# A hybrid attention and retention block on one core: operand halves loaded and split in place, ten gate tiles, a second projection in smaller pieces, and three small moves of order

## Chip, cores and metric

The kernel runs on one core of one Trainium2 chip. The metric is the device time of one execution in microseconds (us). The core has five engines that work side by side, each on its own queue of instructions in a fixed order: TensorE (PE) multiplies matrices, VectorE (DVE) and ScalarE (ACT) work on elements, GpSimd (POOL) takes some small work, and SyncE (SP) issues the transfers (DMA). Engines wait for each other by semaphores. Operands lie in SBUF, PE's results in PSUM, and what does not fit goes to DRAM.

## The reference

One decoder block in float32, 1024 tokens of width 1024:

```python
xn = rmsnorm(x, norm1_g)
qa, ka, va, qr, kr, vr, gr, gate_a, gate_b = split(xn @ w_in)
o_a = dilated window attention (3 groups x 4 heads, mixed)      # S x 512
o_r = head_groupnorm(retention(qr, kr, vr)) * silu(gr)          # S x 2048, 4 heads
y = sigmoid(gate_a) * (o_a @ w_proj_a) + sigmoid(gate_b) * (o_r @ w_proj_b)
x = x + y @ w_out
xn2 = rmsnorm(x, norm2_g)
x = x + square(relu(xn2 @ w_up)) @ w_down
```

The query and key heads are normalised too (`q_norm_g`, `k_norm_g`); that takes a root per head and token.

## The kernel before

**Split operands.** Every float32 operand is split into a high part (`xh`, `wh`, an ACT copy, line 350) and a low part (`xl`, `wl`, the difference, a DVE instruction, line 353). A product takes three matmuls for each pair of 128 rows: high by high, high by low, low by high (line 247, tiles of 128x512).

**Stages.** In order: heads and their norms, attention, retention (four heads of eight chunks, c = 0 to 7), the first projection (`w_proj_a`, tag `pa`), the second (`w_proj_b`, tag `pb`), the output projection, norm, `up`, `down`. The last retention head overlaps with the first projection: PE works on both in turn.

**Products with seven multiplications.** `pb`, `up` and `down` multiply 2x2 blocks with seven products instead of eight (N1 to N7, `product`). The weights of a unit j come as two raw tiles and are split into pieces A, D, B, C; between D and B, DVE makes four sums of raw blocks in place (line 124). On the data side the sums of blocks of the retention's output are made by POOL and DVE, stored in DRAM (`on_d`, line 1021) and read back by halves (512 KB). After N1 ACT copies the result to a second PSUM bank (line 419), after N6 it copies the bank out (line 424), after N7 too (line 427), and PE needs that bank again soon.

**What sets the order.** PE's order is written out by hand. The other engines' instructions are ordered by a scheduler, apart from those that are pinned to the program's order (`keep_in_program_order`). `W` plans the weights: a list of splits, each with a raw load (line 185); `W.lag`, `W.pace` and `W.limit` say how far ahead of use a split is made, and `W.tick`, called after each `pipe.step`, makes the next one. `pipe.at(n, fn)` calls a function n steps later. A tile's load cannot be issued before the last reader of the tile's old content is done; SP's queue waits there, with all that stands behind.

**Buffers around the change.** The attention's output (`oa_d`) and the blocks of the retention's output (`on_d`) are loaded into `oraw` tiles (pool `pr`, three buffers, 512 KB each; lines 905 and 945) and split from there into the operand pairs: `xh_95`/`xl_96`, `xh_97`/`xl_98` (the attention's output), `xh_7928`/`xl_7929` (N5) and `xh_99`/`xl_100` (N7). Until then these pairs hold the normalised input, from which PE makes the last head's values. The gates of the first projection are loaded into `s0` tiles, four in pool `pm2` (line 898, sigmoid in line 909 or 1103, product with PE's result in line 1104, store in line 1105); later ones into pieces of an operand's tile that is not yet needed (`spare`). In the second projection parts for the later half of the units are loaded as quarters (256 KB) into `s` tiles, up to six under way, and split three products later; its results pass through `result`, which adds and multiplies with a gate, and `keep`, which splits them as operands of the output projection.

**Heads' root.** Line 821 takes the square root of the mean squares of four heads at once (`work<-mean`). Root and sigmoid (line 862) are in different tables of ACT, so each change of function loads a table.

Of the kernel before, what the change touches and what calls it, by code (L numbers as in the profile page):

```python
# [17 lines left out]
P = 128  # L18
# [19 lines left out]
class Weights:  # L38
# [38 lines left out]
    def add(self, src, buf=None):  # L77
# [10 lines left out]
        def step():  # L88
            h, l = self.buffer(buf)
            self.split(h[:, :w], l[:, :w], self.raw[r][:, :w])  # L90
            self.units[n] = h, l
            self.used.add(r)
# [4 lines left out]
    def add_units(self, tag, srcs, flip=0):  # L97
# [8 lines left out]
        def piece(key, buf, r, cols, then=None):  # L106
            def step():
# [6 lines left out]
                self.split(h, l, self.raw[r][:, cols], key[0] == "up" and key[1] < 2 and key[2] != "A")  # L114
# [6 lines left out]
        def sums(r):  # L121
            (x22, x21), (x11, x12) = ((self.raw[i][:, 0:512], self.raw[i][:, 512:1024]) for i in (r, r - 1))
            for x, y in ((x22, x21), (x21, x11), (x11, x22), (x12, x11)):
# [106 lines left out]
class Pipe:  # L230
# [25 lines left out]
    def step(self, ps, terms, ends=None, first=True):  # L256
# [14 lines left out]
        self.tick()  # L271
# [25 lines left out]
def hybrid_block(ctx: ExitStack, tc: tile.TileContext, a: dict, out: bass.AP):  # L297
# [51 lines left out]
    def split(dst_h, dst_l, src, pin=False):  # L349
# [3 lines left out]
        nc.vector.tensor_tensor(dst_l, src, dst_h.bitcast(F), op=OP.subtract)  # L353
# [34 lines left out]
    for nb in range(2):  # L388
        for u in range(4):
            W.add(a["w_out"][nb, u], (4, 3, 5, 2)[u] if nb else (0, 1, 5, 2)[u])  # L390
# [9 lines left out]
    def product(tag, j, name, unit, operands, pu, result):  # L400
# [13 lines left out]
        pipe.step(u[bank], terms, None, fresh)  # L414
# [378 lines left out]
    with ExitStack() as ph:  # L793
# [16 lines left out]
        def add(n):  # L810
# [6 lines left out]
            if n == HEADS - 1:  # L817
# [3 lines left out]
                nc.scalar.activation(w, y, AF.Sqrt)  # L821
# [79 lines left out]
    def load_sum(from_, c, name, h):  # L901

        raw = from_.tile([P, 2, 512], F, name="oraw")
        o = 2 * SUMS.index(name)
        nc.sync.dma_start(raw, on_d[2 * c + h, o:o + 2].rearrange("k p t -> p k t"))
        return raw

# [3 lines left out]
    def part_sum(to, raw, h):  # L911

        split(*(x[:, 2 * h:2 * h + 2] for x in to), raw, True)

    ret = ExitStack()
    with ExitStack() as ph:
# [26 lines left out]
        def load_oa(s):  # L943
            raw = pr.tile([P, S], F, name="oraw")
# [3 lines left out]
        for h in range(RH):  # L948
# [4 lines left out]
            for c in range(NT):  # L953
# [119 lines left out]
                if h == RH - 1 and c == NT - 1:  # L1073
                    W.lag, W.pace = 2, 1
                    raws = [(name, g, load_sum(pr, 0, name, g), -3) for name, g in (("N5", 0), ("N5", 1), ("N7", 0))]


    with ExitStack() as ph:
        ES, e1, exts = None, ExitStack(), ExitStack()
        OPB = [{"N5": XS[0, 1], "N7": XS[1, 1]}, {}]  # L1080
        waiting = [("N7", 1)] + [(name, h) for name in ("N1", "N2", "N4", "N6") for h in range(2)]
        spare = []
        sigmoid(gates[0])
        for n, (d, cs) in enumerate(work):
# [6 lines left out]
            for _ in range(2 if len(gates) < n + 8 else 0):  # L1091
                if spare:
                    e, es = work[len(gates)]
                    gates.append(spare.pop(0))
                    nc.sync.dma_start(gates[-1], sg_d[0, e, :, es])
# [3 lines left out]
            if n < len(work) - 1:  # L1099
                s0 = gates[n + 1]  # L1100
                if s0 in places:
                    gates[n + 1] = pm2.tile([P, 512], F, name="s0")
                tc.keep_in_program_order(nc.scalar.activation(gates[n + 1], s0, AF.Sigmoid))
            nc.vector.tensor_tensor(gates[n], gates[n], pp, op=OP.mult)
            nc.sync.dma_start(pa_d[d, :, cs], gates[n])
            if ES is None and not pipe.due:
# [5 lines left out]
                places = [x[:, k].bitcast(F) for x in ES[3] for k in range(4)]  # L1112
                spare = list(places)
# [3 lines left out]
            if raws and raws[0][0] in OPB[0] and raws[0][3] <= n - 2:  # L1117
                name, h, raw, _ = raws.pop(0)
                part_sum(OPB[0][name], raw, h)
            if waiting and waiting[0][0] in OPB[0] and (n % 2 or n > 11) and len(raws) < 3:  # L1120
                name, h = waiting.pop(0)
# [515 lines left out]
```

## Time and profile before

| | |
|---|---|
| three runs | 2178.85, 2179.03, 2179.24 us; median 2179.03 |
| profiled execution | 2176.74 us, its span 2175.0 us |
| PE busy, granted clock | 2151.6 us (99%), full |
| DVE, ACT, POOL busy | 1356.0, 1098.4, 316.0 us |
| data moved by DMA | 358.81 MB, mean 165 GB/s |

By stage, from windows of the profile (us from the span's start):

| stretch | what runs | length | PE busy | DVE | ACT | DMA share |
|---|---|---|---|---|---|---|
| 400 to 430 | heads' norms | 30 | 29.39 | 17.11 | 14.53 | 0.30 |
| 1195 to 1265 | last retention head from chunk 4 on | 70 | 69.50 | 55.75 | 44.48 | 0.52 |
| 1265 to 1305 | first projection | 40 | 38.53 | 24.77 | 20.08 | 0.88 |
| 1305 to 1450 | second projection | 145 | 140.99 | 116.32 | 78.36 | 0.79 |
| 1450 to 1545 | its end, output projection | 95 | 93.92 | 49.12 | 33.17 | 0.45 |
| 1545 to 1580 | start of up | 35 | 32.97 | 30.25 | 22.72 | 0.25 |
| 1580 to 2175 | up and down | 595 | 589.86 | 400.64 | 311.06 | 0.52 |

A row of the timeline reads: start, duration, engine, line, operation, output<-input, shape, count; in brackets the engine's idle time just before it and what ended it. A row of the list of waits reads: engine, tile and line that waited, what ended the wait; then us in total, times, the longest. Successive matmuls overlap, so their durations add up to more than PE's time.

### The profile page before, as it was taken

What the parts mean: (1) busy time and instruction counts of PE and PEld (TensorE: products, weight loads), DVE (VectorE), ACT (ScalarE), POOL (GpSimd) and SP (SyncE); (2) the same over time, 40 slices, a digit from 0 to 9 for tenths busy, and PEclk for the clock granted to TensorE, in tenths of its full rate; (3) what the DMA queues carried; (4) which work ended last, traced back from release to release, by engine and by line L of the source; (5) the groups of instructions that cost most, each with busy time, mean ns of one, the idle gap of its engine ahead of it and who ended that gap; (6) DMA issues with size and microseconds to landing.
All of it is one profiled execution on the core that took longest, in us unless ns stands there. A gap on an engine that the chain in (4) does not pass through costs nothing. (4 is left out here: it accounts for less than half of the span.)

```text
span 2175.0 us, 28668 instructions
## 1 busy us (share of the span) xinstructions
PE 2151.6 (99%) x9928; PEld 1764.2 (81%) x9928; DVE 1356.0 (62%) x2327; ACT 1098.4 (51%) x2097; POOL 316.0 (15%) x340
## 2 busy tenths in 40 slices
PE   9999999999999999999999999999999999999999
PEld 6887777788888888888888877778788888888887
DVE  5723443565556665657776767783865556788884
ACT  5425555444655554545555655552654545755552
POOL 1000000000000000002123120000000000777773
PEclk9999999999999999999999999999999999999999
DMA  6323333333658676664364487774255556745443
GB/s 210 133 82 93 109 104 102 100 130 120 202 170 241 199 222 191 199 200 140 110 193 121 128 288 268 259 239 154 88 150 160 151 146 204 235 152 191 166 140 107
DMA packets 294579, 358.81 MB, mean 165 GB/s; under 512 B 35025, under 2 KB 202385, under 8 KB 294178
## 3 DMA queue, kind: packets, MB, share of 16 engines
q1 hardware_dynamic: 293890, 356.72, 52.4%
q8 instruction: 78, 1.28, 0.2%
q14 instruction: 67, 0.55, 0.1%
q10 hardware_dynamic: 544, 0.26, 0.0%
HBM read 240.33 MB, written 116.59 MB: 164 GB/s over the span
## 5 line engine op out<-in xcount | busy, mean ns | idle before, releaser
L353 DVE TENSOR_TENSOR wl<-raw,wh 128x1024 fp32r<-128x1024 f32 (+1 forms) x308 | 343.0, 1115 | 462.6 <-ACT wh L350 461.5
L350 ACT ACTIVATE wh<-raw 128x1024 fp32r<-128x1024 f32 (+1 forms) x308 | 296.0, 963 | 297.9 <-PE ms L247 106.6
L247 PE MATMUL mm<-xh,wh 128*128 128x512 f32 x960 | 387.7, 404 | 2.3 <-ACT ms L419 2.2
L247 PE MATMUL mm<-xl,wh 128*128 128x512 f32 x960 | 374.2, 390 | 0.9 <-DVE xl L353 0.9
L247 PE MATMUL mm<-xh,wl 128*128 128x512 f32 x960 | 375.0, 391 | 0.0
L247 PE MATMUL ms<-xh,wh 128*128 128x512 f32 x784 | 318.0, 406 | 4.5 <-ACT u L427 2.9
L247 PE MATMUL ms<-xh,wl 128*128 128x512 f32 x784 | 306.2, 391 | 1.4 <-DVE wl L353 1.4
L247 PE MATMUL ms<-xl,wh 128*128 128x512 f32 x784 | 305.6, 390 | 0.0
L247 PEld LDWEIGHTS mm<-xh,wl 128*128 128x128 f32 x960 | 180.2, 188 | 39.6 <-DVE wl L353 0.7
L247 PEld LDWEIGHTS mm<-xh,wh 128*128 128x128 f32 x960 | 180.5, 188 | 37.4 <-ACT ms L419 3.0
L247 PEld LDWEIGHTS mm<-xl,wh 128*128 128x128 f32 x960 | 180.7, 188 | 35.3 <-DVE xl L353 1.3
L247 PE MATMUL mm<-wh,xh 128*128 128x512 f32 x458 | 186.1, 406 | 0.1
L247 PEld LDWEIGHTS ms<-xh,wh 128*128 128x128 f32 x784 | 147.4, 188 | 45.2 <-issue 10.1
L999 POOL TENSOR_TENSOR st<-st,half 128x1 f32<-128x1 f32 x32 | 25.8, 807 | 1075.6 <-DVE st L998 1075.6
L247 PE MATMUL mm<-wh,xl 128*128 128x512 f32 x458 | 179.6, 392 | 0.9 <-DVE xl L353 0.9
L247 PE MATMUL mm<-wl,xh 128*128 128x512 f32 x458 | 178.5, 390 | 0.0
L247 PEld LDWEIGHTS ms<-xh,wl 128*128 128x128 f32 x784 | 147.1, 188 | 33.7 <-DVE wl L353 1.8
L247 PEld LDWEIGHTS ms<-xl,wh 128*128 128x128 f32 x784 | 147.6, 188 | 26.9
L247 PEld LDWEIGHTS mm<-wh,xl 128*128 128x128 f32 x458 | 86.0, 188 | 20.6 <-DVE xl L353 1.4
L247 PEld LDWEIGHTS mm<-wh,xh 128*128 128x128 f32 x458 | 86.2, 188 | 16.1 <-ACT xh L350 0.6
L247 PEld LDWEIGHTS mm<-wl,xh 128*128 128x128 f32 x458 | 86.5, 189 | 15.7
L247 PE MATMUL ms<-wh,xh 128*128 128x512 f32 x232 | 92.3, 398 | 0.0
(309 smaller groups left out, 3827.9 us busy)
## 6 DMA issues: line engine op xcount, KB each, us to landing
raw<-in_w_up SPq DMA_DIRECT2D x32, 512.0 KB, 3.8
h_d<-s SPq DMA_DIRECT2D x64, 256.0 KB, 4.3
raw<-in_w_down SPq DMA_DIRECT2D x32, 512.0 KB, 3.5
raw<-in_w_aqk_q SPq DMA_DIRECT2D x24, 512.0 KB, 3.5
qk_d<-sg SPq DMA_DIRECT2D x48, 256.0 KB, 3.0
qk<-qk_d SPq DMA_DIRECT2D x24, 512.0 KB, 5.8
rb<-rs_d SPq DMA_DIRECT2D x24, 512.0 KB, 7.1
xh<-h_d SPq DMA_DIRECT2D x11, 896.0 KB, 4.6
```

What stands on the lines that cost most here:

```text
L247: self.nc.tensor.matmul(ps, x, y, start=start, stop=stop, skip_group_check=not first)
L350: hi = nc.scalar.activation(dst_h, src, AF.Copy)
L353: nc.vector.tensor_tensor(dst_l, src, dst_h.bitcast(F), op=OP.subtract)
L999: nc.gpsimd.tensor_tensor(st[:, 9:10], st[:, 8:9], half[:, 0:1], op=OP.pow)
```

## The change

1. **Operand parts split in place.** The pool `pr` goes. A half (`load_half`, and `load_oa`) is loaded into the low tile of its own target and split from there: `xh <- xl`, then `xl <- xl - xh`. The splits are pinned and made three steps after the load's step.
2. **Ten gate tiles.** `pm2` has ten buffers; all gates are loaded into them, up to eight ahead, and the sigmoid always writes in place.
3. **Finer second projection.** Its parts come as halves like the others, one a product. For units j > 1 the four sums are made two at a time, and the splits are pinned. The weights' tick comes after the parts of a product have been dealt with, not inside it; the lag is 3. The last results' steps are pinned or held back to the end (`last`).
4. **Heads' root behind a copy.** The root is made one step later, pinned; reciprocals and what follows too.
5. **Up's third weight piece later.** The limit before `up` is one lower and is raised at (0, N2).
6. **Pacing ended sooner.** `W.lag` and `W.pace` are reset in `up` at the last unit but one, N6.

```diff
@@ add_units @@
+                late = key[0] == "pb" and key[1] > 1
-                self.split(h, l, self.raw[r][:, cols], key[0] == "up" and key[1] < 2 and key[2] != "A")
+                self.split(h, l, self.raw[r][:, cols], late or key[0] == "up" and key[1] < 2 and key[2] != "A")
...
+                fine = tag == "pb" and j > 1
-                piece((tag, j, "D"), (self.D, j % 2), r, slice(0, 512), lambda r=r: sums(r))
+                piece((tag, j, "D"), (self.D, j % 2), r, slice(0, 512), None if fine else lambda r=r: sums(r))
+                if fine:
+                    self.steps += [(set(), r, lambda r=r, k=k: sums(r, k)) for k in ((0, 1), (2, 3))]
@@ the heads' norms @@
-                nc.scalar.activation(w, y, AF.Sqrt)
+                pipe.at(1, lambda: tc.keep_in_program_order(nc.scalar.activation(w, y, AF.Sqrt)))
...
-                    pipe.at(2 + c, lambda c=c: invert(slice(P * c, P * c + P)))
-                pipe.at(6, refine)
+                    pipe.at(3 + c, lambda c=c: invert(slice(P * c, P * c + P)))
+                pipe.at(7, refine)
@@ loads of the parts @@
-    def load_sum(from_, c, name, h):
-
-        raw = from_.tile([P, 2, 512], F, name="oraw")
-        o = 2 * SUMS.index(name)
-        nc.sync.dma_start(raw, on_d[2 * c + h, o:o + 2].rearrange("k p t -> p k t"))
-        return raw
...
-    def part_sum(to, raw, h):
-
-        split(*(x[:, 2 * h:2 * h + 2] for x in to), raw, True)
+    def load_half(at, c, name, h):
+
+        xh, xl = (x[:, 2 * h:2 * h + 2] for x in OPB[c][name])
+        o = 2 * SUMS.index(name)
+        nc.sync.dma_start(xl.bitcast(F), on_d[2 * c + h, o:o + 2].rearrange("k p t -> p k t"))
+        begun.append((at, xh, xl))
+
+    def split_halves(upto):
+
+        while begun and begun[0][0] <= upto:
+            _, xh, xl = begun.pop(0)
+            split(xh, xl, xl.bitcast(F), True)
...
-            raw = pr.tile([P, S], F, name="oraw")
+            raw = oaS[s][1].bitcast(F)
...
-                    pr = pool(load, "pr", 3)
-                    pm2 = pool(load, "pm2", 4)
+                    pm2 = pool(load, "pm2", 10)
...
-                    raws = [(name, g, load_sum(pr, 0, name, g), -3) for name, g in (("N5", 0), ("N5", 1), ("N7", 0))]
+                    for name, g in (("N5", 0), ("N5", 1), ("N7", 0)):
+                        load_half(-3, 0, name, g)
@@ first projection, step n @@
-            if len(gates) == n + 3 and n + 3 < len(work):
-                e, es = work[n + 3]
+            while len(gates) < min(n + 8, len(work)):
+                e, es = work[len(gates)]
                 gates.append(loaded(pm2, sg_d[0, e, :, es], "s0"))
...
-                s0 = gates[n + 1]
-                if s0 in places:
-                    gates[n + 1] = pm2.tile([P, 512], F, name="s0")
-                tc.keep_in_program_order(nc.scalar.activation(gates[n + 1], s0, AF.Sigmoid))
+                sigmoid(gates[n + 1])
...
+            split_halves(n - 3)
+            if waiting and waiting[0][0] in OPB[0] and (n % 2 or n > 11):
+                load_half(n, 0, *waiting.pop(0))
@@ second projection @@
+            if n == len(results) - 1 and n in ahead and not done:
+                done.append(n)
+                last.append(lambda: result(j, f, cs, src))
+                return
...
+            elif j > 5 and cs.start and n < len(results) - 1:
+                last.append(lambda: keep(j, f, cs, y))
...
+        W.lag = 3
...
             product("pb", j, name, unit, OPB[j // 4], lambda: parts, result)
-            todo += [(1, after[j, name], k) for k in range(4) if (j, name) in after]
+            pipe.tick()
+            todo += [(1, after[j, name], h) for h in range(2) if (j, name) in after]
...
+            split_halves(base + i - 3)
+            if todo:
+                load_half(base + i, *todo.pop(0))
@@ before and in up @@
-    W.limit = W.first["up"] + 5
+    W.limit = W.first["up"] + 4
...
-            if (j, name) in ((1, "N2"), (0, "N5")):
-                W.limit = W.limit + 1 if j else len(W.steps) - 11 * (NC - 1)
+            if (j, name) in ((0, "N2"), (1, "N2"), (0, "N5")):
+                W.limit = W.limit + 1 if name == "N2" else len(W.steps) - 11 * (NC - 1)
...
+            if (j, name) == (NU - 2, "N6"):
+                W.lag, W.pace = 0, None
```

PE's and POOL's instructions keep their order. In what follows a line number of the changed kernel stands some 5 to 13 above that of the same line before (350 becomes 356, 994 becomes 1007). First ACT in the heads' norms, before and after (`work<-mean` is the root, `u<-ms` the copy after N7, `sg<-` the sigmoids):

```order
L350 ACTIVATE wh_3067<-raw_2789 128x1024
L821 ACT_TABLE_LOAD
L821 ACTIVATE work<-mean 128x512
L427 ACTIVATE u_3048<-ms 128x512
L862 ACT_TABLE_LOAD
L862 ACTIVATE sg<-u_3048 128x512
L862 ACTIVATE sg<-mm 128x512
```

```order
L356 ACTIVATE wh_3067<-raw_2789 128x1024
L435 ACTIVATE u_3047<-ms 128x512
L870 ACTIVATE sg<-u_3047 128x512
L829 ACT_TABLE_LOAD
L829 ACTIVATE work<-mean 128x512
L870 ACT_TABLE_LOAD
L870 ACTIVATE sg<-mm 128x512
```

The copy and one sigmoid now stand ahead of the root and its table load.

Second, ACT at the end of the last retention head, before and after (`on` is the copy of the head's output that is normalised, `Sh` the state's high part, `smh` that of the scores, `onT` the transposed output, `s0` a gate's sigmoid):

```order
L350 ACTIVATE xh_7928<-oraw_11258 128x1024
L994 ACTIVATE on_11200<-ms_11190 128x512
L350 ACTIVATE Sh_11222<-St_10410 128x512
L350 ACTIVATE wh3_11378<-raw2_11176 128x512
L350 ACTIVATE Sh_11222<-St_10410 128x512
L1103 ACTIVATE s0_11036<-s0_11036 128x512
L350 ACTIVATE smh_11239<-sm_11237 128x128
L350 ACTIVATE vh_11250<-mm_11140 128x512
L350 ACTIVATE xh_7928<-oraw_11260 128x1024
L350 ACTIVATE wh5_11425<-raw0_11182 128x512
L1031 ACTIVATE onT_11278<-tr_11273,gng_106 128x128 x4
L1103 ACTIVATE s0_11138<-s0_11138 128x512
```

```order
L356 ACTIVATE xh_7928<-xl_7929 128x1024
L1007 ACTIVATE on_11194<-ms_11184 128x512
L356 ACTIVATE xh_7928<-xl_7929 128x1024
L356 ACTIVATE wh3_11376<-raw2_11170 128x512
L356 ACTIVATE Sh_11216<-St_10407 128x512 x2
L910 ACTIVATE s0_11031<-s0_11031 128x512
L356 ACTIVATE vh_11244<-mm_11134 128x512
L356 ACTIVATE wh5_11420<-raw0_11176 128x512
L910 ACTIVATE s0_11132<-s0_11132 128x512
L356 ACTIVATE xh_99<-xl_100 128x1024
L356 ACTIVATE smh_11233<-sm_11231 128x128
L1044 ACTIVATE onT_11272<-tr_11267,gng_106 128x128 x4
```

The split of N5's second half has moved ahead of the state's parts, and that of N7's first half, which stood behind `onT` and a sigmoid, ahead of `smh`.

Third, SP in the same place, before and after:

```order
L185 DMA raw0_11182<-in_w_pa 128x512
L185 DMA raw1_11337<-in_w_pa 128x512
L1021 DMA on_d_85<-onE_10736 128x4x128
L1021 DMA on_d_85<-onT_11152 128x4x128
L1021 DMA on_d_85<-n6_11158 128x2x128
L905 DMA oraw_11389<-on_d_85 128x2x512
```

```order
L919 DMA xl_7929<-on_d_85 128x2x512
L190 DMA raw0_11176<-in_w_pa 128x512
L919 DMA xl_7929<-on_d_85 128x2x512
L1034 DMA on_d_85<-onE_10733 128x4x128
L1034 DMA on_d_85<-onT_11146 128x4x128
L1034 DMA on_d_85<-n6_11152 128x2x128
L190 DMA raw1_11331<-in_w_pa 128x512
L919 DMA xl_100<-on_d_85 128x2x512 x2
```

Before, the load in this place was that of N7's second half; N5's halves and N7's first had been issued between chunks 4 and 6. Now all four stand here, each behind PE's last reading of its target.

More of the change, by code (lines that the diff above doesn't have):

```diff
@@ L254, in group, with step @@
                 after(i)
-    def step(self, ps, terms, ends=None, first=True):
+    def step(self, ps, terms, ends=None, first=True, tick=True):
         fns = self.due.pop(self.slot, [])
@@ L1087, in hybrid_block @@
                 uh, ul = W[ua]
-            if len(gates) == n + 3 and n + 3 < len(work):
-                e, es = work[n + 3]
+            while len(gates) < min(n + 8, len(work)):
+                e, es = work[len(gates)]
                 gates.append(loaded(pm2, sg_d[0, e, :, es], "s0"))
[L1091 to L1095, printed above, removed]
+                if len(gates) > n + 5:
+                    break
             pp = ms.tile([P, 512], F, name="ms")
@@ L1154, in fetch, with keep @@
             ahead[n] = [loaded(pm3, src[d, :, cs], "s") for src in srcs]
-        def keep(j, f, cs, y):
+        last, done = [], []
+        def keep(j, f, cs, y, pin=False):
             yh, yl = (x[:, f, cs] for x in as_rows(YS[j - 4]))
-            split(yh, yl, y)
+            split(yh, yl, y, pin, pin)
         def result(j, f, cs, src):
@@ L1191, in hybrid_block @@
         fetched = {order[order.index(at) - 3]: u for at, u in free.items()}
-        todo, unit = [(c, name, k) for c, name in ((0, "N3"),) for k in range(4)], {}
-        begun = []
-        def load_part(c, name, k):
-            return loaded(pm3, on_d[2 * c + k // 2, 2 * SUMS.index(name) + k % 2], "s")
+        todo, unit, base = [(0, "N3", h) for h in range(2)], {}, len(work)
+        W.lag = 3
         fetch(0)
@@ L1221, in hybrid_block @@
         W.pump()
+        for fn in last:
+            fn()
         e1.close()
```

54 lines of the change are left out of this document (23 added, 31 removed).

## The prediction

> **What bounds the kernel now.** I read the page's busy time first, then TensorE's (PE's) list of waits, then the timeline round each wait.
>
> ```profile
> span 2175.0 us, 28668 instructions
> PE 2151.6 (99%) x9928; PEld 1764.2 (81%) x9928; DVE 1356.0 (62%) x2327; ACT 1098.4 (51%) x2097; POOL 316.0 (15%) x340
> PE ms L247 <- ACT u L427: 2.9, 4, 1.2
> PE mm L247 <- ACT ms L419: 2.2, 2, 1.4
> PE mm L247 <- DVE xl L353: 1.8, 2, 0.9
> PE ms L247 <- DVE s L1104: 1.5, 2, 1.2
> PE ms L247 <- DVE wl L353: 1.4, 1, 1.4
> ```
>
> PE is busy 99% of the span, and the change leaves its instructions and their order as they are. So only PE's waits can move the time. The five rows add up to 9.8 us; that is nearly all that this change can touch and win. The profiled execution took 2176.74 us, 1.74 more than its span and 2.29 less than the median of the runs, 2179.03. I make the sum on 2176.74 and carry the difference to the median. A shift under 0.2% (4.4 us) I count as no change.
>
> After a wait the next 128x512 matmul takes 0.50 us where its neighbours take 0.39 (rows below), so removing a wait wins its length and 0.1.
>
> **Gains, part by part.** *The heads' root.*
>
> ```profile
> 416.36 1.28 ACT L821 ACT_TABLE_LOAD   x1
> 417.66 0.63 ACT L821 ACTIVATE work<-mean 128x512 f32<-128x512 f32 x1
> 418.19 0.58 ACT L427 ACTIVATE u<-ms 128x512 f32<-128x512 f32 x1
> 418.82 0.50 PE L247 MATMUL ms<-xh,wh 128*128 128x512 f32 x1 [0.61 <-ACT u L427]
> ```
>
> ScalarE (ACT) takes table load and root ahead of the copy at L427 that empties PE's accumulator. Afterwards the copy and one sigmoid stand first. What is late then is the root, and its readers (reciprocals on VectorE, DVE) are moved one step later too. Gain 0.6 + 0.1 = 0.7.
>
> *Ten gate tiles.* In the first projection a gate's sigmoid (L1103) and product (L1104) wait until an earlier store frees their tile:
>
> ```profile
> 1285.68 0.63 ACT L1103 ACTIVATE s<-xh 128x512 f32<-128x512 f32 x1 [2.69 <-DMA pa_d<-s]
> 1286.34 0.69 DVE L1104 TENSOR_TENSOR s<-s,ms 128x512 f32<-128x512 f32 x1 [2.09 <-ACT s L1103]
> 1287.08 0.50 PE L247 MATMUL ms<-xh,wh 128*128 128x512 f32 x1 [1.23 <-DVE s L1104]
> ```
>
> With ten tiles the sigmoids run in place and no store stands in front; the last gates are loaded six steps ahead. Both waits on L1104 go: 1.5 + 2 x 0.1 = 1.7.
>
> *Operand splits, second projection.* Its start and its two waits on L427 look alike: splits stand ahead of the copy that PE needs.
>
> ```profile
> 1306.69 1.06 ACT L350 ACTIVATE xh<-oraw 128x1024 fp32r<-128x1024 f32 x1 [0.25 <-DMA oraw<-on_d]
> 1307.66 1.06 ACT L419 ACTIVATE ms<-mm 128x512 f32<-128x512 f32 x2
> 1308.29 0.50 PE L247 MATMUL mm<-xh,wh 128*128 128x512 f32 x1 [1.35 <-ACT ms L419]
> 1328.05 0.50 PE L247 MATMUL ms<-xh,wh 128*128 128x512 f32 x1 [0.41 <-ACT u L427]
> 1405.86 0.50 PE L247 MATMUL ms<-xh,wh 128*128 128x512 f32 x1 [0.70 <-ACT u L427]
> ```
>
> Afterwards only one split, of a part loaded some 3 us before, stands ahead of L419, with about 1 us to spare: gain 1.4. At 1328 the split moves behind the copy: 0.5. At 1405.86 a split of 128x1024 (1.06) replaces two of half that size, but a weight's split no longer stands ahead of it; I leave 0.2 of the wait and take 0.6.
>
> *Finer second projection.* The low half of a weight waits in DVE's queue:
>
> ```profile
> 1438.79 0.69 DVE L353 TENSOR_TENSOR xl<-s,xh 128x512 fp32r<-128x512 f32 x1
> 1439.40 2.36 DVE L353 TENSOR_TENSOR wl<-raw,wh 128x1024 fp32r<-128x1024 f32 x2
> 1440.67 0.50 PE L247 MATMUL ms<-xh,wl 128*128 128x512 f32 x1 [1.42 <-DVE wl L353]
> 1466.16 0.50 PE L247 MATMUL mm<-wh,xl 128*128 128x512 f32 x1 [0.94 <-DVE xl L353]
> ```
>
> With the sums drawn apart, 11 half-size DVE steps (the first row and the next start 0.61 apart), ACT's split (1.06) and the low half (half of 2.36) follow the product that starts them: 6.7 + 1.1 + 1.2 = 9.0. PE's 38 matmuls up to this weight's use take 38 x 0.23 = 8.7 (one starts 0.23 after the other in the timeline). I leave 0.4 of the wait and take 1.1. At the output projection's start the last weight splits end about 3 us before PE needs the results' low halves: the wait of 0.94 and a small one before it go, 1.2.
>
> Gains: 0.7 + 1.7 + 1.4 + 0.5 + 0.6 + 1.1 + 1.2 = 7.2. If the tight places keep half their waits it is 5.5; with none left, 8.0.
>
> **Edits that I cost at nothing.** *Up's third weight piece.*
>
> ```profile
> 1559.39 1.99 ACT L350 ACTIVATE wh<-raw 128x1024 fp32r<-128x1024 f32 x2
> 1562.92 0.49 PE L247 MATMUL mm<-xh,wh 128*128 128x512 f32 x1 [0.83 <-ACT ms L419]
> 1562.17 2.35 DVE L353 TENSOR_TENSOR wl<-raw,wh 128x1024 fp32r<-128x1024 f32 x2
> 1573.40 0.69 DVE L1267 TENSOR_TENSOR x<-x,x 128x512 f32<-128x512 f32 x1
> 1574.66 1.07 ACT L1360 ACTIVATE q<-mm 128x512 f32<-128x512 f32 x2
> 1575.29 0.49 PE L247 MATMUL mm<-xh,wh 128*128 128x512 f32 x1
> ```
>
> The second of the two splits moves behind the copies at L419, so PE starts 0.9 sooner at 1562. But from 1562.17 to the addition that ends at 1574.09 DVE has no gap, and its work up to there is the same in another order. ACT's squares (L1360) still begin at 1574.66 behind a split of that addition, and PE, ahead by 0.9, waits for them at 1575.29. The gain is given back: 0, with 0.9 as the upper end.
>
> *Pacing ended sooner.* Nothing moves in any queue from there on. The wait that it could have meant stays:
>
> ```profile
> 1861.14 0.50 PE L247 MATMUL ms<-xh,wh 128*128 128x512 f32 x1 [1.15 <-ACT u L427]
> ```
>
> **Losses: the loads into the operands themselves.** Before, halves came into a ring of their own, long before their split. Now a load writes the low operand's tile, and SyncE (SP) may issue it only when PE has finished with that tile. The splits stand in ACT's and DVE's in-order queues at nearly the old places, ahead of the last retention head's own steps.
>
> ```profile
> oraw<-on_d SPq DMA_DIRECT2D x6, 512.0 KB, 4.0
> DMA to landing us min/median/max: 3.7/5.0/6.0
> 1198.72 1.04 ACT L350 ACTIVATE xh<-oraw 128x1024 fp32r<-128x1024 f32 x1
> 1202.78 0.58 ACT L994 ACTIVATE on<-ms 128x512 f32<-128x512 f32 x1
> 1213.08 0.61 ACT L994 ACTIVATE on<-ms 128x512 f32<-128x512 f32 x1
> 1243.07 0.60 ACT L994 ACTIVATE on<-ms 128x512 f32<-128x512 f32 x1
> 1248.14 0.45 SPq L905 DMA_DIRECT2D oraw<-on_d  x1
> 1248.54 0.31 ACT L350 ACTIVATE smh<-sm 128x128 fp32r<-128x128 f32 x1
> 1249.11 0.63 PE L1026 MATMUL tr<-ident,on 128*128 128x128 f32 x4
> 1253.54 0.60 ACT L994 ACTIVATE on<-ms 128x512 f32<-128x512 f32 x1
> ```
>
> I take 4.0 us from issue to landing, the median for this stretch (first row), with 3.7 and 6.0 as ends.
>
> *Chunks 4 and 5.* PE frees the first target near 1198.7, where the split used to start. Load and split end near 1204, so the normalising copy (L994) ends at about 1204.6 instead of 1203.4. About 1.2 us of slack follow before PE transposes it, leaving 0.3. In chunk 5 two splits, a gate's sigmoid and its table load stand ahead of the copy at 1213.08: it slips by some 2.2 against a slack of 0.8, leaving 1.4. Together 1.7; ends 0.5 and 3.6.
>
> *The end of the head.* The first half of N5 is issued after PE's read near 1239.1, lands near 1243, and its split pushes the copy of 1243.07 to 1244.5. DVE, with both halves' low parts (1.23 each) ahead of the normalisation, is ready for the transposes of 1249.11 about 1.3 late; 0.1 of this stood there before. The first half of N7 stands in SP's queue behind three stores and a weight load, is issued near 1248.7 and lands near 1252.7. Its split stands in ACT's queue ahead of `smh` of 1248.54, `onT` and the copy of 1253.54, which then ends near 1256.3 where PE wants it near 1255.2 (already slipped); behind it the gate product and both low halves of the state are late by 0.7, 0.4 and 0.5. In all 1.2 + 1.1 + 0.7 + 0.4 + 0.5 = 3.9, less 0.4 of waits that were there: 3.5; ends 2.2 and 6.4.
>
> Losses 1.7 + 3.5 = 5.2; 2.7 to 10.0.
>
> [...]
>
> **Sum.** 2176.74 - 7.2 + 5.2 = 2174.7 for an execution like the profiled one; plus 2.29, 2177.0 for the median.
>
> **Rivals.**
>
> 1. *The loads land soonest and hurt little* (faster). If they land in 3.7 us and each split keeps its slack, the losses are 2.7, the gains 8.0, and the time is 2179.03 - 5.3 = 2173.7. For it: SP and the DMA engines are not full in this stretch. Against it: one load stands behind three stores, and two waits are DVE's order rather than the landing.
> 2. *The late loads decide* (slower). The place is ACT's queue at the end of the last retention head. If the halves land at 6.0, the longest row, they cost 10.0; with the gains at 5.5 the time is 2179.03 + 4.5 = 2183.5. It decides from the point where the seven loads cost more than what the second projection gives back with the rest, 7.2. For it: stores, weights and halves are in flight together. Against: the six loads of this stretch landed at a median of 4.0.
> 3. *The up stage keeps its gain* (the change does more than I credit): 0.9 off, 2176.1. DVE's row without a gap speaks against it. The opposite, that pacing does nothing, is in the forecast already.
>
> **How the numbers follow.** The forecast, with rival 3 in it, has 0.54, rival 1 0.29, rival 2 0.17. The likeliest is 2177.0. Its own bounds are 2179.03 - 8.0 - 0.9 + 2.7 = 2172.8 and, with central gains and the highest loss, 2179.03 - 7.2 + 10.0 = 2181.8; reaching a little into the rivals I give 2172.0 to 2183.0. Rival 1 lies wholly below the 0.2% line; most of rival 2 lies within it unless the gains are small too, but what I could not price (the second projection's in-place loads) would add on its side, so I leave it 0.15. Faster 0.30, same 0.55, slower 0.15.
>
> **What would show it.** Right: no PE wait near 418.8, on L1104, on L419 at the second projection's start or on `wl` near 1440; new PE waits of about 1.3 before the transposes (L1026) of chunks 5 and 7 and of about 1 behind the copy at L994, with ACT idle on a DMA ahead of `xh<-xl`; a wait near 1 us on L1360 at the up stage's start; the wait of 1.15 before `u` in the down stage unchanged. Wrong: no idle time in the last retention head (then rival 1), waits over 6 us there (rival 2), or new waits in the second projection on halves that have not landed.

## Result and profile after

| | before | after |
|---|---|---|
| median of 10 runs each, on one chip | 2178.93 us | 2185.68 us (2180.98 to 2188.52) |
| ratio, 95% interval | | 1.0026 (1.0018 to 1.0035) |
| profiled execution, its span | 2176.74, 2175.0 us | 2186.4, 2184.6 us |
| mean granted clock of PE | 1.000 | 0.998 |

The change made the kernel slower by 0.26%. It was predicted at 2177.0, within 2172 and 2183, with slower given 0.15. Both the time and its sign were wrong.

PE's order is the same in both kernels, so its matmuls can be laid side by side one by one. The table gives how far the profiled execution of after has fallen behind that of before at each place, and what each stretch added.

| place (time in before) | behind, us | added here | predicted |
|---|---|---|---|
| start, attention (0 to 40, 850 to 950), not touched | | +2.1 | 0 |
| heads' root (419) | 1.3, these two together | -0.8 | -0.7 |
| last retention head, chunks 4 to 7 (1208 to 1258) | 6.9 | +5.6 | +5.2 |
| gates (1287, 1296) | 5.2 | -1.7 | -1.7 |
| second projection's start (1308) | 7.6 | +2.4 | -1.4 |
| its N7 copies (1328, 1386, 1406), drift between | 5.2 | -2.3 | -1.1 |
| near 1410 | 10.9 | +5.7 | 0 |
| low half of a weight (1438, 1441) | 10.6 | -0.4 | -1.1 |
| output projection's start (1464, 1466), drift | 8.9 | -1.7 | -1.2 |
| start of up (1546 to 1603) | 9.6 | +0.7 | 0 |
| rest | 9.65 | +0.1 | 0 |

The first row is no effect of the change: waits at the same places came out differently from one execution to the next (one near 37 is 1.08 us in after and 1.6 in `free` below, and does not stand in before). The views here and below show chosen rows. The first is the page's busy time of after and then PE's list of waits in after (engine, tile, line, what ended the wait; us in total, times, longest).

```profile
span 2184.6 us, 28560 instructions
PE 2154.3 (99%) x9928; PEld 1767.8 (81%) x9928; DVE 1354.2 (62%) x2311; ACT 1095.2 (50%) x2081; POOL 314.7 (14%) x340
PE tr L1039 <- DVE on L1014: 3.3, 6, 1.1
PE mm L252 <- ACT xh L356: 2.6, 1, 2.6
PE mm L252 <- ACT ms L427: 2.2, 1, 2.2
PE ms L252 <- ACT on L1007: 1.6, 1, 1.6
PE mm L252 <- DVE wl L359: 1.4, 1, 1.4
PE ms L252 <- ACT u L435: 1.3, 2, 1.0
PE ms L252 <- DVE s L1109: 0.8, 1, 0.8
PE ms L252 <- DVE Sl L359: 0.6, 1, 0.6
```

ACT and DVE do slightly less than before (3.2 and 1.8 us). PE is idle for 30.3 us of the span instead of 23.4, and it is busy 2.7 us longer with the same matmuls, because its clock was lower for a while (below). The waits on `xh` (L356), on `Sl` and, ahead of `mm`, on `wl` (L359) have no line in the list of before, and the two on `on` were shorter there (1.2 and 0.3).

**The last retention head.** PE's waits, in the timeline of after:

```profile
1210.70 0.66 PE L1039 MATMUL tr<-ident,on 128*128 128x128 f32 x4 [0.53 <-DVE on L1014]
1252.88 0.63 PE L1039 MATMUL tr<-ident,on 128*128 128x128 f32 x4 [1.07 <-DVE on L1014]
1259.29 0.50 PE L252 MATMUL ms<-vh,kzh 128*128 128x512 f32 x1 [1.64 <-ACT on L1007]
1261.06 0.50 PE L252 MATMUL ms<-xh,wh 128*128 128x512 f32 x1 [0.81 <-DVE s L1109]
1264.24 0.50 PE L252 MATMUL ms<-Sl,qh 128*128 128x512 f32 x1 [0.60 <-DVE Sl L359]
```

ACT's rows before the first of them and before the third:

```profile
1204.14 1.06 ACT L356 ACTIVATE xh<-xl 128x1024 fp32r<-128x1024 f32 x1 [2.09 <-DMA xl<-oa_d]
1205.10 0.58 ACT L1007 ACTIVATE on<-ms 128x512 f32<-128x512 f32 x1
1256.10 1.06 ACT L356 ACTIVATE xh<-xl 128x1024 fp32r<-128x1024 f32 x1 [2.94 <-DMA xl<-on_d]
1257.06 0.30 ACT L356 ACTIVATE smh<-sm 128x128 fp32r<-128x128 f32 x1
1258.63 0.60 ACT L1007 ACTIVATE on<-ms 128x512 f32<-128x512 f32 x1
```

ACT stands idle for 2.09 and 2.94 us until a load has landed, and the head's own copy (L1007) comes behind its split. What was loaded is not needed for a long time; PE needs the copy at once.

**The second projection's start.** SP's loads, ACT and PE in after's timeline:

```profile
1304.96 1.06 SPq L919 DMA_DIRECT2D xl<-on_d  x2
1309.42 1.06 ACT L356 ACTIVATE xh<-xl 128x1024 fp32r<-128x1024 f32 x1 [2.11 <-DMA xl<-on_d]
1310.38 1.04 ACT L356 ACTIVATE wh<-raw 128x1024 fp32r<-128x1024 f32 x1
1311.33 1.04 ACT L356 ACTIVATE xh<-xl 128x1024 fp32r<-128x1024 f32 x1
1312.71 1.06 ACT L356 ACTIVATE xh<-xl 128x1024 fp32r<-128x1024 f32 x1 [0.34 <-DMA xl<-on_d]
1313.67 1.06 ACT L427 ACTIVATE ms<-mm 128x512 f32<-128x512 f32 x2
1314.31 0.61 PE L252 MATMUL mm<-xh,wh 128*128 128x512 f32 x1 [2.22 <-ACT ms L427]
1314.71 0.63 PE L252 MATMUL mm<-xl,wh 128*128 128x512 f32 x1
```

The wait was to go, and grew from 1.35 to 2.22. The split at 1312.71 starts when its half lands; SP issued that load as the second of the two in the first row, near 1305.5, so it took some 7.2 us. The prediction had it loaded some 3 us before. That last landing alone held ACT up for 0.34 us. The splits ahead had been held up already: the one at 1309.42 waited 2.11 for another half (issued at 1303.95, landed some 5.4 us later), and from there to the copy (L427) four splits stand in a row.

**Near 1418, where before had no wait.** First ACT in after's timeline:

```profile
1409.99 0.62 ACT L910 ACTIVATE s<-s 128x512 f32<-128x512 f32 x1
1415.48 0.63 ACT L356 ACTIVATE xh<-s 128x512 fp32r<-128x512 f32 x1 [4.87 <-DVE s L1181]
1416.02 1.04 ACT L356 ACTIVATE wh<-raw 128x1024 fp32r<-128x1024 f32 x1
1416.96 1.04 ACT L356 ACTIVATE xh<-xl 128x1024 fp32r<-128x1024 f32 x1
```

Then DVE there:

```profile
1408.89 2.35 DVE L359 TENSOR_TENSOR xl<-xl,xh 128x1024 fp32r<-128x1024 f32 x2
1411.16 0.68 DVE L436 TENSOR_TENSOR u<-u,mm 128x512 f32<-128x512 f32 x1
...
1414.76 0.69 DVE L1181 TENSOR_TENSOR s<-s 128x512 f32<-128x512 f32 x1
```

And PE:

```profile
1418.05 0.50 PE L252 MATMUL mm<-xh,wh 128*128 128x512 f32 x1 [2.58 <-ACT xh L356]
1419.50 0.50 PE L252 MATMUL mm<-xl,wh 128*128 128x512 f32 x1 [0.95 <-DVE xl L359]
```

PE waits for the split of a half (1416.96). No transfer is late: this half had landed near 1408. ACT is idle for 4.87 us, because the split of a *result* (`xh<-s`, 1415.48) stands ahead in its queue, and the half's split is pinned, so that the scheduler may not put it in front. (The result's own split is not pinned in the kernel.) The result comes out of a chain that keeps DVE busy without a gap from 1408.89 to 1415.45.

**The clock behind these two waits.** Windows of after (us; busy time and count of PE, PEld, DVE, ACT, POOL; granted clock; DMA share; GB/s):

```profile
1300.00:1314.00 14.00, 12.09 (x54) 9.60 (x52) 11.62 (x15) 9.51 (x12) 0.00 (x0) 1.00 0.94 325
1314.00:1318.00 4.00, 3.69 (x9) 2.91 (x10) 4.00 (x5) 1.71 (x3) 0.00 (x0) 0.57 1.01 393
1318.00:1322.00 4.00, 4.00 (x19) 3.28 (x19) 3.27 (x6) 2.21 (x3) 0.00 (x0) 1.00 0.86 324
1420.00:1424.00 4.00, 4.00 (x13) 3.13 (x12) 3.90 (x7) 1.67 (x3) 0.00 (x0) 0.57 0.74 250
1424.00:1430.00 6.00, 6.00 (x28) 4.97 (x27) 4.78 (x8) 3.03 (x5) 0.00 (x0) 1.00 0.57 171
```

Behind the waits of 2.22 and 2.58 about 8 matmuls start 0.43 apart instead of 0.23, and the granted clock is 0.57. That costs 8 x 0.2 = 1.6 us each time, on top of the wait. The first row is the stretch in which the late half was under way: the DMA engines were busy for 0.94 of it.

**Start of up.** PE and DVE in after:

```profile
1577.53 0.68 DVE L359 TENSOR_TENSOR xl<-x,xh 128x512 fp32r<-128x512 f32 x1
1578.13 1.22 DVE L359 TENSOR_TENSOR wl<-raw,wh 128x1024 fp32r<-128x1024 f32 x1
1579.40 0.50 PE L252 MATMUL mm<-xh,wl 128*128 128x512 f32 x1 [1.43 <-DVE wl L359]
1870.59 0.50 PE L252 MATMUL ms<-xh,wh 128*128 128x512 f32 x1 [1.02 <-ACT u L435]
```

The wait of 0.83 on L419 went, and one of 1.43 on the low half of the moved piece came. The last row is the wait in down that the pacing could have touched: 1.15 before, 1.02 now.

### The profile page after: what moved, and what is told of

The parts are those of the page before. It is cut to its first block, busy times and chain, and to the rows that moved or that the text cites. A ratio compares the mean times of both kernels' runs of the same rounds, so it can differ in the third digit from the quotient of the medians.

```text
span 2184.6 us, 28560 instructions
## 1 busy us (share of the span) xinstructions
PE 2154.3 (99%) x9928; PEld 1767.8 (81%) x9928; DVE 1354.2 (62%) x2311; ACT 1095.2 (50%) x2081; POOL 314.7 (14%) x340
## 4 chain that ended last, share of the span: by engine, by line
PE 50%; DVE 4%; issue 2%; DMA 2%; POOL 1%; ACT 1%; SPq 0%; POOLq 0%; ACTq 0%; DVEq 0%
PE mm L252 28%; PE ms L252 20%; DVE xl L359 1%; PE tr L1039 1%; PE ms L979 0%; DVE wl L359 0%; POOL st L1012 0%; DMA rkT<-rqk_d 0%; ACT xh L356 0%; DMA rb<-rs_d 0%; DMA xl<-on_d 0%; DVE Y L1465 0%; PE tr L692 0%; ACT wh L356 0%; POOL n L1054 0%
## 5 line engine op out<-in xcount | busy, mean ns | idle before, releaser
L359 DVE TENSOR_TENSOR wl<-raw,wh 128x1024 fp32r<-128x1024 f32 (+1 forms) x308 | 342.8, 1114 | 465.0 <-ACT wh L356 464.2
L356 ACT ACTIVATE wh<-raw 128x1024 fp32r<-128x1024 f32 (+1 forms) x308 | 296.3, 962 | 281.0 <-PE ms L252 99.7
```

What stands on the lines that cost most here:

```text
L356: hi = nc.scalar.activation(dst_h, src, AF.Copy)
L359: lo = nc.vector.tensor_tensor(dst_l, src, dst_h.bitcast(F), op=OP.subtract)
```

## Experiments

Ratios are against before on the same chip, with 95% intervals; single executions are named as such.

**Root alone (`root`).** Before with the root edit only:

```diff
-                nc.scalar.activation(w, y, AF.Sqrt)
+                pipe.at(1, lambda: tc.keep_in_program_order(nc.scalar.activation(w, y, AF.Sqrt)))
...
-                pipe.at(6, refine)
+                pipe.at(7, refine)
```

> The kernel before with the heads' root alone behind the copy. Theory: the wait of 0.61 near 418.8 goes, 0.7 us with the slow matmul behind it, and no other wait between 400 and 560 appears. Rival (the root's readers are late in its place): a new wait on L1039's like or on VectorE between 420 and 560.

One execution, 2176.42 us. The 0.61 wait at 418.8 is gone, PE gains 0.77 there, and no new wait follows between 420 and 560. This part does what was predicted.

**The old ring in the last head (`ring`).** After, with `pr` (three buffers), `pm2` (four), `load_sum` and `part_sum` of before up to the end of the first projection; the second projection as in after:

```diff
-                    pm2 = pool(load, "pm2", 10)
+                    pr = pool(load, "pr", 3)
+                    pm2 = pool(load, "pm2", 4)
...
-            raw = oaS[s][1].bitcast(F)
+            raw = pr.tile([P, S], F, name="oraw")
...
```

> The changed kernel, but the last retention head and the first projection as before the change: halves and attention's output through a ring of three tiles, four gate tiles. Theory: the waits in chunks 4, 5 and 7 of the changed kernel (5.3 us) shrink to the 0.5 of before, and the gates' waits of 1.23 and 0.24 come back; the start of the second projection waits 1 to 1.6. Rival (something else in the change, the gates or the order of weights, causes the waits in the head): at least 2 us of them stay.

2181.13 us, ratio 1.0011 (1.0002 to 1.0021). No new wait in chunks 4 to 7; the gates' wait is back. The waits near 1412 (2.58 and 0.95) stay. So the last head's losses come from its loads and buffers (this run takes the ten gate tiles back as well), and those near 1418 do not come from the head.

**Splits of N5 and N7 later (`later`).** After with

```diff
-                        load_half(-3, 0, name, g)
+                        load_half(2, 0, name, g)
```

> The changed kernel, but the halves of N5 and N7's first, loaded at the end of the last retention head, are split five steps of the first projection later; their loads stay where they are. Theory (a split that waits for its load stands in ScalarE's and VectorE's in-order queues ahead of the head's own steps): the waits of chunk 7 in the changed kernel (1.07 before the transposes, 1.64 behind the copy L1007, 0.81 behind L1109, 0.60 and 0.09 behind Sl, 4.2 us in all) fall to 0.6 or less, the time by 3.5 to 4.5 us. Rival (the loads themselves, or ten gates' loads, hold up the head's own transfers): at least 3 us of these waits stay. Chunks 4 and 5 (0.53 and 0.52) stay in either.

2181.40 us, ratio 1.0014 (1.0004 to 1.0024). The loads are issued as in after; only the splits stand five steps later. PE's list of waits in this kernel:

```profile
PE ms L252 <- DVE s L1109: 1.7, 1, 1.7
```

ACT in its timeline:

```profile
1280.64 1.06 ACT L356 ACTIVATE xh<-xl 128x1024 fp32r<-128x1024 f32 x1 [2.80 <-DMA xl<-on_d]
```

All waits of chunk 7 are gone; those of chunks 4 and 5 (0.81, 0.54), from the attention's halves, stay. But the splits now stand close together in the first projection, and one, waiting 2.80 for a later half, blocks a gate's sigmoid: 1.7 us. The time falls by about 2.6 us from after (ratio 1.0026 to 1.0014), less than the 3.5 to 4.5 expected. The place of the split in the queue sets the loss, and a new place must be chosen too.

**Second projection by quarters (`quarters`).** After, with that projection's parts loaded into tiles of their own and split unpinned, by before's lines:

```diff
-            todo += [(1, after[j, name], h) for h in range(2) if (j, name) in after]
+            todo += [(1, after[j, name], k) for k in range(4) if (j, name) in after]
...
-            split_halves(base + i - 3)
-            if todo:
-                load_half(base + i, *todo.pop(0))
+            while begun and begun[0][0] <= i - 3:
...
```

> The changed kernel, but the second projection's parts are loaded by quarters into tiles of their own and split from there without a pin, as before the change; all else stays. Theory (pinned splits of halves that had to wait for their target stand at a fixed place in the queues, ahead of or behind work that PE needs): the waits of 2.58 and 0.95 near 1418 go, and with them the eight slow matmuls behind them; the wait of 2.2 at the second projection's start falls to 1.4 or less; together 5 to 8 us. Rival (the sums drawn apart and the late splits of the weights make VectorE late there): at least 2 us of wait stay near 1418, and the time falls by less than 3 us.

2179.49 us, ratio 1.0008 (0.9998 to 1.0017). The waits near 1418 are gone and that at the start is 0.27. Part of it comes back elsewhere: 1.88 us at 1409.3 on L435, behind splits of quarters that waited for their landing, with 8 matmuls at half clock after it. So the time falls by some 4 us from after (ratio 1.0026 to 1.0008), not by the 5 to 8 expected.

**Halves, but unpinned (`free`).** After with

```diff
-    def split_halves(upto):
+    def split_halves(upto, pin=True):
...
-            split(xh, xl, xl.bitcast(F), True)
+            split(xh, xl, xl.bitcast(F), pin)
...
-            split_halves(base + i - 3)
+            split_halves(base + i - 3, False)
```

> The changed kernel, but the splits of the halves in the second projection are not pinned, so that the scheduler may place them. Theory (the pin puts them there): the waits of 2.58 and 0.95 near 1418 fall below 1 in all. Rival (the halves come too late, because each load waits until its target is free; the pin does no harm): they stay above 2 in all.

2180.68 us, ratio 1.0008 (0.9999 to 1.0017). The 2.58 and 0.95 near 1418 are gone with the pin alone, the loads in place as in after; the wait of 0.24 on a weight's high half that after has near 1450 grows to 1.04 (at 1444.7 here). At the projection's start a wait of 2.0 stays.

**Up's limit as before (`limit`).** After with

```diff
-    W.limit = W.first["up"] + 4
+    W.limit = W.first["up"] + 5
...
-            if (j, name) in ((0, "N2"), (1, "N2"), (0, "N5")):
+            if (j, name) in ((1, "N2"), (0, "N5")):
```

> The changed kernel with the limit before up as it was. Theory (VectorE is full there, so that the move of the third piece only moves the wait): the wait of 1.43 on wl near 1579 goes and 0.83 on L427 near 1570 comes back; this stage is 0.3 to 0.7 us shorter than in the changed kernel. Rival (the move won 0.9 and the wait of 1.43 has another cause): the wait on wl stays and the stage is 0.9 longer.

One execution, 2180.34 us. The 1.43 on `wl` is gone and the 0.83 on L427 is back; the start of up is some 0.4 shorter than in after. At the second projection's start, up to which this program is the same as after, PE waits 0.79 instead of 2.22 and the clock stays up, with a landing of 6.6 us instead of 7.2: that wait varies from one execution to the next.

**Waits of growing length (`clock`).** Before, with

```diff
-            nc.scalar.activation(u["u3"], ps, AF.Copy)
+            for _ in range(j + 2 if tag == "up" and 3 <= j <= 12 else 1):
+                nc.scalar.activation(u["u3"], ps, AF.Copy)
```

The repeats write the same values.

> The kernel before, but in up the copy after N7 (L427) is made 5, 6, ... 14 times for the units 3 to 12, so that PE's waits there grow from unit to unit by about 0.48 us, from none to about 4.6. Theory (after a wait over some 2 us PE's clock is granted at about half for some 1.7 us): behind waits up to 1.7 the matmuls start 0.23 apart at once, behind waits over 2.2 about eight start 0.43 apart, with about 1.6 us lost, whatever the length. Rival (the slow matmuls of the changed kernel come from the DMA traffic at those places): all matmuls behind these waits start 0.23 apart. Third way: the loss grows with the wait.

One execution, 2246.59 us. The waits came out longer than expected, from 1.55 to 7.6 in steps of 0.63 behind the second. Windows behind the waits of 1.55, 2.56 and 4.45:

```profile
1642.00:1646.00 4.00, 3.11 (x14) 2.57 (x15) 0.69 (x1) 2.90 (x6) 0.00 (x0) 1.00 0.58 199
1664.80:1668.80 4.00, 4.00 (x11) 3.19 (x12) 0.65 (x1) 1.26 (x2) 0.00 (x0) 0.61 0.49 131
1738.90:1743.00 4.10, 4.08 (x10) 3.21 (x11) 0.69 (x1) 1.26 (x2) 0.00 (x0) 0.50 0.22 64
```

The lower clock came with little and with much transfer: 0.61 and 0.50 at DMA shares of 0.49 and 0.22 here, 0.57 at 1.01 and 0.74 in after; at 0.58 here it was 1.00. That it lasts some 1.7 us, as the theory had it, was not shown: in after the slow matmuls go from 1314.31 to 1317.70, 3.4 us. The time lost to matmuls that start more than 0.23 apart does not grow steadily with the wait; it lay between 1.5 us (behind 3.82) and 2.7 us (behind 5.08), not at 1.6 whatever the length.

**All placements mended (`fix`).** After with the edits of `free` and `limit`, and

```diff
-            split(*oaS[s], raw)
+            split(*oaS[s], raw, True)
...
-                    for name, g in (("N5", 0), ("N5", 1), ("N7", 0)):
-                        load_half(-3, 0, name, g)
+                    for at, name, g in ((0, "N5", 0), (2, "N5", 1), (4, "N7", 0)):
+                        load_half(at, 0, name, g)
```

> The changed kernel with four places moved: the splits of the attention's output pinned to the program's order (one a chunk, so later), those of N5 and N7 spread over steps 3, 5 and 7 of the first projection, those of the second projection's halves not pinned, and up's limit as before. Theory (every loss came from where splits of just-loaded halves stand, the rest of the change is a gain): no wait over 0.3 us in chunks 4 to 7, none over 0.6 near 1314 and 1418, the wait of 1.43 on wl at up's start gone and that of 0.83 on L427 back; no slow matmuls behind a wait; the time 4 to 7 us below the kernel before. Rival (the loads themselves come too late for any place): waits of more than 3 us in all stay between 1200 and 1420, and the time is no better than before.

2173.48 us, ratio 0.9976 (0.9967 to 0.9985): 5.5 us faster than before, with every load in place as in after. (The splits of the attention's output, first edit, are not pinned in after; the section on the change says so of all.) Chunks 4 to 6 have no wait and chunk 7 one of 0.29; the second projection starts with one of 0.38 and has one of 0.62 on a weight's low half 7 us on. What is left of the loss is near 1438, PE in the timeline of this kernel:

```profile
1436.62 0.50 PE L252 MATMUL ms<-xh,wh 128*128 128x512 f32 x1 [1.25 <-ACT wh L356]
1437.88 0.50 PE L252 MATMUL ms<-xh,wl 128*128 128x512 f32 x1 [0.53 <-DVE wl L359]
1438.46 0.43 PE L252 MATMUL ms<-xl,wh 128*128 128x512 f32 x1
1438.69 0.63 PE L252 MATMUL ms<-xh,wl 128*128 128x512 f32 x1
1439.11 0.63 PE L252 MATMUL ms<-xh,wh 128*128 128x512 f32 x1
...
1442.10 0.39 PE L252 MATMUL ms<-xl,wh 128*128 128x512 f32 x1
```

No single wait here is over 1.25 us, and yet eight matmuls start 0.43 apart, from 1438.69 to 1442.10, and the granted clock is 0.53 (window 1438.6 to 1442.2). That was not expected: the theory had no slow matmuls left.

**What is left near 1438 (`pinned2`, `whole`, `unpinned`).** Each is `fix` with one edit, in this order:

```diff
-            split_halves(base + i - 3, False)
+            split_halves(base + i - 2)
```
```diff
-                fine = tag == "pb" and j > 1
+                fine = False
```
```diff
-                late = key[0] == "pb" and key[1] > 1
+                late = False
```

> The kernel 'fix', but the second projection's halves are pinned again, and split two products after their load instead of three. Theory (the wait near 1418 of the changed kernel comes from the pinned half standing behind a result's split that waits for VectorE; a product earlier it stands in front): no wait over 1 near 1410, and the wait of 1.25 near 1436 of 'fix' back at 0.2; 2 us faster than 'fix'. Rival (two products, some 5.5 us, are too little for the landing): new waits on xh<-xl behind a DMA, over 1.5 us in all, and no gain over 'fix'.

> The kernel 'fix', but the four sums of raw blocks of a unit are made in one step of the plan again, as before the change. Theory (the finer sums are what brings the wait of 1.42 on wl near 1440 down to 0.5): it comes back, 1 us or more longer than in 'fix'. Rival (the sums apart only shift waits): the second projection from 1400 to 1470 takes as long as in 'fix' to within 0.5 us, or less.

> The kernel 'fix', but the splits of the second projection's weights for units above 1 are not pinned, as before the change. Theory (the late pinned splits hold VectorE's sums back near 1436, where 'fix' waits 0.62 + 1.25 + 0.53 and then loses 1.6 by the slower clock): these waits fall below 1 in all and the slow matmuls go; 2 to 3 us faster than 'fix'. Rival (the pins keep the weights' splits from getting in the way of PE's copies): waits on L427 or L435 of over 1.5 us in all appear elsewhere in the second projection, and it is no faster.

| | median, us | ratio, 95% interval | waits in the second projection |
|---|---|---|---|
| `pinned2` | 2173.97 | 0.9972 (0.9960 to 0.9983) | none near 1410; 1.63 and 0.91 near 1438 |
| `whole` | 2171.57 | 0.9963 (0.9948 to 0.9978) | 0.65 at 1345; 1.26 and 0.53 near 1438 |
| `unpinned` | 2173.28 | 0.9970 (0.9957 to 0.9982) | 0.53 at 1328; 1.69 at 1387; 0.52 near 1438 |

The intervals of all four versions overlap, so none of the gains over `fix` that were expected shows. In `pinned2` the half's split does stand in front near 1410, but the wait near 1436 grew instead of going. In `unpinned` the waits near 1436 went, and 1.69 came elsewhere, as its rival said. Halves split two products after their load may even stay pinned; the weight's late low half (1.42 in before) is 0.53 with whole sums as well, against the theory of `whole`. So neither finer sums nor the pin of the weights is worth anything that shows here; they shift waits. In `unpinned` it reads, in PE's timeline:

```profile
1386.76 0.50 PE L252 MATMUL ms<-xh,wh 128*128 128x512 f32 x1 [1.69 <-ACT u L435]
```

**Waits of three lengths (`window`).** Before, with

```diff
-            nc.scalar.activation(u["u3"], ps, AF.Copy)
+            for _ in range(5 + j % 3 if (tag == "up" and 3 <= j <= 14) or tag == "down" else 1):
+                nc.scalar.activation(u["u3"], ps, AF.Copy)
```

> Before with the copy after N7 (L427) made five, six or seven times in up's units 3 to 14 and in every unit of down; the repeats change nothing in the values. Waits of PE of about 1.6, 2.4 and 3.1 us, some 24 us apart, are expected, and a time some 40 to 80 us longer. [...]

One execution, 2223.98 us; 32.2 us of waits on the copy. In up every wait of 2.56 and 3.19 was followed by 7 or 8 matmuls at half clock, none of 1.56; two longer ones in down (3.31 and 3.99) by 12 and 6. The granted clock was 1.00 around a wait of 1.56 (window 1641 to 1645), 0.62 behind one of 2.56 (1664.6 to 1668.6) and 0.58 behind one of 3.19 (1688.8 to 1692.8). Here every wait on the copy of over 2 us was followed by slow matmuls; `fix` has them behind shorter ones, as the last section shows.

## Why the prediction was wrong

**Right, by their own terms.** The root (-0.7; -0.8). The gates on L1104 (-1.7; -1.7). The copies L427 at 1328 and 1406 (-1.1; -1.4). The waits of the output projection's start (-1.2; -1.4 without drift). The last head's losses (5.2; 5.6), with ACT idle on a DMA ahead of `xh<-xl` and the copy behind it, as foretold; the waits on L1014 in chunks 4 and 5 came as 0.53 and 0.52 rather than 0.3 and 1.4, and those at the head's end as 1.07, 1.64, 0.81 and 0.60. Pacing: nothing. Up's gain of 0.9 was given back, though on `wl` and not on L1360, and some 0.4 beyond it.

**Right in number, not in mechanism.** The low half `wl` has 0.53 left where 0.4 was expected, but `whole` has 0.53 without the finer sums, so that the sums drawn apart are not shown to be the reason; and a new wait of 0.24 just ahead of it leaves -0.4 of the -1.1.

**The step that failed** is "Operand splits, second projection". For its start the prediction said "only one split, of a part loaded some 3 us before, stands ahead of L419, with about 1 us to spare: gain 1.4". In the trace that load took 7.2 us and another 5.4, in a stretch with a DMA share of 0.94, and four splits stood in a row ahead of the copy, not one. The prediction names no landing time here; its "3 us before" would fit the 4.0 that it took for the last head (share 0.52). Yet its own longest row, 6.0, is a load at this very place: in before it is issued at 1300.65 and ends just ahead of the split at 1306.69. Instead of -1.4 came +0.9 and a stretch at half clock, +1.5: a miss of 3.8. Inside the projection, the halves loaded and split in place were given no term at all; the text named them only as "what I could not price". There stood 2.58 + 0.95 of new waits and again a stretch at half clock: a miss of 5.7. Together 9.5, of which some 3 are the half clock, for which the prediction's price of a wait (its length and 0.1) has no term. The profiled execution came out 9.65 above before; without the 2.1 of the untouched places that is 7.5, where -2.0 (the sum 2174.7 less 2176.74) was predicted: a miss of 9.5. The two places account for it.

`free` and `quarters` show what made the second place: unpinned, or from tiles of their own, the splits do not wait behind a result's split, and the 2.58 and 0.95 are gone. It could have been bounded: the result's split stands ahead of the half's in the changed kernel's queue on ACT, and the trace of before shows the chain of the results on DVE (L1176 to L1181, from 1407.27 on) that must end first.

**The rival on the slower side** had the right sign for the wrong reason: it needed landings of 6 us in the last head, and the head lost what the forecast said. The landings were that long one stage later, at the second projection's start.

**Not shown.** How much of the miss near 1308 belongs to that one execution: its wait was 2.22 in after, 0.79 in `limit`, 1.11 in `ring`, 0 in `later`. Old ring and ten gate tiles together were not run.

## What to carry to other kernels

Loading into the operand itself cost little here; what cost was the place of the consuming split in an in-order queue. A split that waits for a landing (2.94 us on ACT at 1256.10 in after), or for a long chain on another engine (4.87 us at 1415.48), holds up whatever stands behind it, needed or not, and a pin keeps the scheduler from putting the needed one in front: here moving splits, with all loads in place and the edit to up undone, turned some 6.7 us lost into 5.5 us won. And when a term cannot be priced for want of a row, read the new order for what stands ahead of each instruction that the bounding engine needs, and give the term a bound, rather than a nought.

`fix` is faster than before without the extra buffers (2173.48 us, ratio 0.9976): the end of its last head has one wait of 0.29 where before, with its ring, has 0.14 and 0.32. So here the place of the split did what the extra buffers had done.

## What the runs showed of the hardware

**The granted clock behind waits of PE, from 1250 us on.** Places are us from the span's start. The clock is that of the window in brackets, or the mean of the run.

| run, place | PE's waits there, us | matmuls behind | granted clock |
|---|---|---|---|
| `clock`, 1642.89 | 1.55 | 0.23 apart | 1.00 (1642 to 1646) |
| after, 1259.29 and 1261.06 | 1.64, 0.81 | 0.23 apart | 1.00 (1259 to 1263) |
| `unpinned`, 1386.76 | 1.69 | 0.23 apart | 1.000 (run) |
| `pinned2`, near 1438 | 1.63, 0.91 | none slow | 1.000 (run) |
| `fix`, 1436.62 and 1437.88 | 1.25, 0.53 | eight 0.43 apart | 0.53 (1438.6 to 1442.2) |
| `quarters`, 1409.30 | 1.88 | 0.43 apart from 1410.83 on | 0.999 (run) |
| after, 1314.31 | 2.22 | about eight 0.43 apart | 0.57 (1314 to 1318) |
| `clock`, 1664.79 | 2.56 | 0.43 apart from 1665.98 on | 0.61 (1664.8 to 1668.8) |
| after, 1418.05 and 1419.50 | 2.58, 0.95 | about eight 0.43 apart | 0.57 (1420 to 1424) |

So the length of the longest wait does not tell the two cases apart: in `fix` the clock fell behind waits of 1.25 and 0.53, and in `pinned2` and after it stayed at 1.00 behind 1.63 and 1.64. Nor does the sum of neighbouring waits: 1.25 and 0.53 make 1.78, while 1.63 and 0.91 make 2.54 and 1.64 and 0.81 make 2.45. What does tell them apart was not shown. For the price of a wait that leaves two measured cases: its length and 0.1, or some 1.6 more where the clock fell (8 x 0.2 in after; 1.5 to 2.7 in `clock`).
